# Every fourth weight tile of the first layer's experts: its second part subtracted on GpSimd instead of VectorE

## The chip, the core and the metric

The kernel runs on one core of a Trainium2 chip. Its engines work side by side, each through its own queue of instructions in program order: TensorE (PE in the profile) multiplies matrices out of SBUF into PSUM, VectorE (DVE) and ScalarE (ACT) do elementwise work, GpSimd (POOL) does elementwise work and issues indirect DMAs, SyncE (SP) issues the other DMAs. They wait for each other by semaphores. The metric is the device time of one execution in microseconds (us); before the change it is 3566.11 us, the median of three runs (3563.67 to 3567.10).

## The reference, cut to what matters

The program is two transformer blocks of two layers each, on 256 tokens of width 1024. The second block's feed-forward is a layer of 16384 experts (128 x 128). For each token, eight heads score 128 + 128 sub-keys, the best 16 of each side are combined, the best 16 sums are chosen, and the 16 experts per head are mixed:

```python
def peer_block(hb, w_q, sub_keys, u_tab, v_tab):
    ...
    top_s, pos = lax.top_k(cand_s, PEER_TOPK)
    expert = jnp.take_along_axis(cand_i, pos, axis=-1)
    g = jax.nn.softmax(top_s, axis=-1)
    u = u_tab[expert]
    act = jax.nn.gelu(jnp.einsum('nhkd,nd->nhk', u, hb).astype(jnp.float32))
    w = (g * act).astype(hb.dtype)
    return jnp.einsum('nhk,nhkd->nd', w, v_tab[expert])
```

In the first of the two layers 256 latent tokens and 256 context tokens go through it.

## The kernel before

The kernel doesn't gather experts for most tokens: it runs all 16384 experts densely, as 128 tiles of 128 experts, and multiplies with a gate matrix that is zero where an expert wasn't chosen. In the first layer (l = 0) 448 tokens go this way (N = ND = 448); the other 64 context tokens go through `gather`, which fetches two rows of experts per step with an indirect DMA from GpSimd (L1329) and multiplies them on VectorE (L1338 for `u`, L1344 for `v`). The second layer has N = S = 256 tokens.

A float32 matrix is used as two float32r parts, so that three matmuls give the precision of one float32 product: `split` writes the first part on ScalarE (L210, a copy that rounds) and the second on VectorE (L211, the source minus the first part), and `mac` issues first x first (L244), first x second (L245) and second x first (L246). A weight tile of 128 x 1024 thus costs one ScalarE and one VectorE instruction of 1024 columns, and 24 matmuls.

The first pass is `ahead`: for each tile e, `hidden` loads `u[e]` (buffer tag `w`, four buffers), splits it into two `ws` buffers of four, multiplies it with h into PSUM tag A, applies the GELU (L1146), and the result goes to DRAM (`kept`). Tiles 0 to 26 have 256 columns here, since their context half was done earlier (`fill`); tiles 27 to 127 have 448. With four `ws` buffers the parts of tile e + 2 can be written only after the matmuls of tile e.

Beside it `ahead` steps through side work at given rates: `key_scores` and `choose` (VectorE: top-16, L945 to L1043), `spread`, which builds the gate matrix, and the gather. `spread` makes a one-hot tile for every four tokens: three instructions on GpSimd and one on VectorE (L1078), three more on VectorE (L1082), eight small matmuls (L1096), a copy on ScalarE (L1097); 112 such tiles in this layer. Their buffers are the three of tag `wb`, which the loads of `v` and of the modulation weights use too.

The second pass is `experts`: for each tile, `weigh` loads `kept[e]` and `v[e]`, splits `v[e]` into a `k8` buffer of seven, multiplies the activation with its gate (L1192), splits that, and `sums` issues 24 matmuls, one tile behind, into eight PSUM banks.

The functions record instructions in program order; a scheduler of the framework then sets each engine's order by its own estimates of durations. Here are the functions around the change, with the line numbers of the profile.

Of the kernel before, what the change touches and what calls it, by code (L numbers as in the profile page):

```python
# [10 lines left out]
F32 = mybir.dt.float32  # L11
# [4 lines left out]
ALU = mybir.AluOpType  # L16
AX = mybir.AxisListType

P = 128
S = 256  # L20
D = 1024
KC = 8
# [36 lines left out]
class Net:  # L59
# [145 lines left out]
            return tuple(t if t is None or b is None else t[:, b * P:(b + 1) * P] for t in dst(k))  # L205
        return hT

    def split(self, hi, lo, src):

        self.nc.scalar.copy(hi, src)  # L210
        self.nc.vector.tensor_sub(lo, src, hi.bitcast(F32))  # L211

    def cut_in_two(self, shape, raw):

        tag = self.ring[self.turn % len(self.ring)]
        self.turn += 1
        if tag == "ws":
            hi, lo = self.t("ws", [P] + shape, F32R), self.t("ws", [P] + shape, F32R)
        else:
            both = self.t(tag, [P, 2] + shape, F32R)  # L220
            hi, lo = both[:, 0], both[:, 1]
        self.split(hi, lo, raw)
        return hi, lo

    def weights(self, sd, src, n=512, order=None):
# [906 lines left out]
    def hidden(self, l, e, h, N, aside=False):  # L1132

        nc, io = self.nc, self.io
        raw = self.load("wb" if aside else "w", [P, KC, P], io["u"][l, e])
        if aside:
            both = self.t("b8", [P, 2, KC, P], F32R)
            uh, ul = both[:, 0], both[:, 1]
            self.split(uh, ul, raw)
        else:  # L1140
            uh, ul = self.cut_in_two([KC, P], raw)
        pA = self.p("B" if aside else "A", [P, N])
        for k in range(KC):
            self.mac(pA, (uh[:, k], ul[:, k]), h(k), k == 0, k == KC - 1)
        ge = self.t("b2" if aside else "k2", [P, N])
        nc.scalar.activation(ge, pA, AF.Gelu_apprx_tanh)  # L1146
        return ge
# [24 lines left out]
    def experts(self, l, h, N, Gd, kept, side, home):  # L1172

        nc, io = self.nc, self.io
        m = 8
        pv = [self.p(t, [P, 512 if N == S else N]) for t in ("CCCC" if N == S else "CCCCBBAA")]
        Gs = None

        def weigh(e):
            nonlocal Gs
            c, j = divmod(e, m)
            if j == 0:
                Gs = self.t(home, [P, N // NT, m, NT])
                nc.sync.dma_start(Gs, Gd[:, :, m * c:m * c + m])
            ge = self.load("k2", [P, N], kept[e]) if e < kept.shape[0] else self.hidden(l, e, h, N)
            raw = self.load("wb", [P, D], io["v"][l, e])
            vs = self.t("k8", [P, 2, D], F32R)
            self.split(vs[:, 0], vs[:, 1], raw)  # L1190
            g3 = ge.rearrange("p (n t) -> p n t", t=NT)
            nc.vector.tensor_mul(g3, g3, Gs[:, :, j])  # L1192
            ws = self.t("k4", [P, 2, N], F32R)
            self.split(ws[:, 0], ws[:, 1], ge)
            return ws, vs

        def sums(i, e, ws, vs):
            w, v = ([t[:, j] for j in range(2)] for t in (ws, vs))
            if N == S:
                b, d = divmod(i, 2)  # L1200
                self.mac(pv[i], self.cut(w, b * P, (b + 1) * P), self.cut(v, 512 * d, 512 * d + 512), e == 0, e == 127)
            else:
                self.mac(pv[i], self.cut(v, i * P, (i + 1) * P), w, e == 0, e == 127)

        banks, late = range(len(pv)), []
        last = None
        for e in range(129):
            if side is not None:
                side(e)
            new = (e,) + weigh(e) if e < 128 else None  # L1210
            if e > 128 - TAIL:
                late.append(last)
            elif last is not None:
                for i in banks:
                    sums(i, *last)
            last = new
        for i in banks:
            for w in late:
                sums(i, *w)
            yield i, pv[i]  # L1220
# [345 lines left out]
```

## Time and profile before

| | |
|---|---|
| median of 3 runs | 3566.11 us (3563.67 to 3567.10) |
| the profiled execution, its span | 3569.61 us, 3567.2 us |
| TensorE matmul busy | 3375.9 us (95%) |
| VectorE, ScalarE busy | 2466.8 us (69%), 1508.8 us (42%) |
| GpSimd busy | 748.7 us (21%), in two stretches: `spread` of each layer |
| granted TensorE clock, mean | 0.976 |

The shares are means over stages with different limits. A stage is read from its own window: who is busy there, and for whom TensorE waits. A row of the grouped lines gives line, engine, operation, tiles written and read, shapes and count, then busy us, mean ns of one, and the idle time of the engine before them with what ended it. A row of the timeline gives start, duration, engine, line, and in brackets the idle time before it and its releaser.

### The profile page before, as it was taken

The page shows a single profiled execution, that of the slowest core. Times are in us where ns is not written, and L with a number is a line of the kernel's source. Part 1 is how long each engine was busy: PE and PEld are TensorE (multiplying, and loading weights), DVE is VectorE, ACT ScalarE, POOL GpSimd, SP SyncE. Part 2 cuts the span into 40 slices and gives each one's busy share as a digit, 9 for nine tenths or more (in the row PEclk, how much of TensorE's full clock was granted, in tenths as well). Part 3 has the DMA queues.
Part 4 walks back from the last instruction along what each step waited for, and adds up shares of the span by engine and source line. Part 5 has one row for each costly group of instructions (what it writes and reads, how often), then busy time and mean ns, then how long its engine had stood idle before and what let it go on. Part 6 is the DMA issues. An engine that isn't in the chain of part 4 may idle for free. (4 is left out here: it accounts for less than half of the span.)

```text
span 3567.2 us, 54493 instructions
## 1 busy us (share of the span) xinstructions
PE 3375.9 (95%) x19896; PEld 2942.5 (82%) x19896; DVE 2466.8 (69%) x5248; ACT 1508.8 (42%) x2556; POOL 748.7 (21%) x728
## 2 busy tenths in 40 slices
PE   8999999999999998999876999999989999999999
PEld 6687777799888987888765889888968999998777
DVE  6656776655667678997756765555477888756666
ACT  6543455444454433433312233233354545555443
POOL 0000000000000055988843200000010045730000
PEclk9999999999999998999998999999999999999999
DMA  7446644455524656776789977786322577788885
GB/s 242 157 159 214 208 152 136 158 201 196 169 92 147 217 198 225 256 246 217 276 302 316 331 261 246 243 251 220 109 67 103 197 243 260 252 288 287 291 273 194
DMA packets 338796, 767.05 MB, mean 215 GB/s; under 512 B 30368, under 2 KB 190624, under 8 KB 332640
## 3 DMA queue, kind: packets, MB, share of 16 engines
q1 hardware_dynamic: 320096, 696.46, 58.0%
q0 software_dynamic: 18432, 67.12, 5.3%
q8 instruction: 156, 2.56, 0.3%
q14 instruction: 112, 0.92, 0.1%
HBM read 668.50 MB, written 94.96 MB: 214 GB/s over the span
## 5 line engine op out<-in xcount | busy, mean ns | idle before, releaser
L210 ACT CAST ws<-w 128x1024 fp32r<-128x1024 f32 (+1 forms) x528 | 547.2, 1036 | 958.1 <-PE psA L245 693.0
L211 DVE TENSOR_TENSOR ws<-w,ws 128x1024 fp32r<-128x1024 f32 (+1 forms) x528 | 637.1, 1207 | 323.5 <-ACT ws L210 320.3
L246 PE MATMUL psA<-b,ws 128*128 128x256 f32 (+1 forms) x2048 | 661.4, 323 | 46.1 <-DVE ws L211 45.8
L244 PE MATMUL psA<-b,ws 128*128 128x256 f32 (+1 forms) x2048 | 667.2, 326 | 0.7 <-ACT k L1146 0.7
L245 PE MATMUL psA<-b,ws 128*128 128x256 f32 (+1 forms) x2048 | 658.0, 321 | 0.0
L1078 POOL TENSOR_SCALAR wb<-iota,R 128x128 f16<-128x128 f16 x528 | 524.3, 1007 | 459.4 <-ACT R L1049 317.6
L210 ACT CAST k<-wb 128x1024 fp32r<-128x1024 f32 x256 | 268.5, 1051 | 484.1 <-DMA wb<-in_v 480.2
L246 PEld LDWEIGHTS psA<-b,ws 128*128 128x128 f32 x2048 | 391.4, 191 | 72.5 <-DVE ws L211 57.7
L244 PE MATMUL psC<-k,k 128*128 128x512 f32 (+1 forms) x1056 | 404.8, 383 | 22.7 <-ACT k L210 22.7
L245 PE MATMUL psC<-k,k 128*128 128x512 f32 (+1 forms) x1056 | 407.0, 385 | 16.2 <-DVE k L211 16.0
L244 PEld LDWEIGHTS psA<-b,ws 128*128 128x128 f32 x2048 | 394.2, 192 | 15.1 <-ACT k L1146 1.1
L246 PE MATMUL psC<-k,k 128*128 128x512 f32 (+1 forms) x1056 | 404.1, 383 | 2.4 <-DVE k L211 2.4
L245 PEld LDWEIGHTS psA<-b,ws 128*128 128x128 f32 x2048 | 391.4, 191 | 14.0
L211 DVE TENSOR_TENSOR k<-wb,k 128x1024 fp32r<-128x1024 f32 x256 | 312.2, 1220 | 74.3 <-ACT k L210 67.8
L159 POOL TENSOR_TENSOR rsrf<-rsvf,neghalf 128x1 f32<-128x1 f32 (+5 forms) x38 | 39.6, 1049 | 1456.0 <-DVE rsvf L158 1454.8
L1192 DVE TENSOR_TENSOR k<-k,b 128x448 f32<-128x448 f32 (+1 forms) x256 | 131.5, 522 | 178.7 <-DMA k<-kept 173.2
L245 PE MATMUL psC<-ws,k 128*128 128x512 f32 (+1 forms) x608 | 242.0, 398 | 5.0 <-DVE ws L211 4.7
L244 PEld LDWEIGHTS psC<-k,k 128*128 128x128 f32 x1056 | 200.1, 190 | 56.5 <-ACT k L210 24.0
L245 PEld LDWEIGHTS psC<-k,k 128*128 128x128 f32 x1056 | 200.4, 190 | 52.4 <-DVE k L211 21.6
L244 PE MATMUL psC<-ws,k 128*128 128x512 f32 (+1 forms) x608 | 241.6, 401 | 0.7 <-ACT ws L210 0.6
L246 PE MATMUL psC<-ws,k 128*128 128x512 f32 (+1 forms) x608 | 238.9, 394 | 0.1
L246 PEld LDWEIGHTS psC<-k,k 128*128 128x128 f32 x1056 | 200.4, 190 | 36.8 <-DVE k L211 5.0
(445 smaller groups left out, 6597.8 us busy)
## 6 DMA issues: line engine op xcount, KB each, us to landing
w<-in_u SPq DMA_DIRECT2D x256, 512.0 KB
wb<-in_v SPq DMA_DIRECT2D x256, 512.0 KB
w<-in_w_ff SPq DMA_DIRECT2D x128, 512.0 KB
G<-k SPq DMA_DIRECT2D x44, 1024.0 KB
wb<-in_ada_w SPq DMA_DIRECT2D x80, 512.0 KB
b<-G SPq DMA_DIRECT2D x16, 1792.0 KB
k<-kept SPq DMA_DIRECT2D x128, 224.0 KB
w<-in_wA SPq DMA_DIRECT2D x48, 512.0 KB
```

The lines of the kernel that those rows point to most:

```text
L159: nc.gpsimd.tensor_tensor(r[:m, :cols], v[:m, :cols], self.neghalf[:m, :cols], op=ALU.pow)
L210: self.nc.scalar.copy(hi, src)
L211: self.nc.vector.tensor_sub(lo, src, hi.bitcast(F32))
L244: self.nc.tensor.matmul(out, ah, bh, start=first, stop=False)
L245: self.nc.tensor.matmul(out, ah, bl, start=False, stop=False)
L246: self.nc.tensor.matmul(out, al, bh, start=False, stop=last)
L1078: eng.tensor_scalar(first[:, j], self.iota16, r0[:, n + j:n + j + 1], None, ALU.is_equal)
L1192: nc.vector.tensor_mul(g3, g3, Gs[:, :, j])
```

## The change

`split` gets a flag `far` that puts its subtraction on GpSimd; `hidden` and `weigh` set it for every fourth tile of the layer with 448 columns (`N > S`). Tiles 0 to 26 of the first pass and the whole second layer keep VectorE. 26 subtractions of `u` and 32 of `v` move.

```diff
-    def split(self, hi, lo, src):
+    def split(self, hi, lo, src, far=False):
 
         self.nc.scalar.copy(hi, src)
-        self.nc.vector.tensor_sub(lo, src, hi.bitcast(F32))
-
-    def cut_in_two(self, shape, raw):
+        (self.nc.gpsimd if far else self.nc.vector).tensor_tensor(lo, src, hi.bitcast(F32), op=ALU.subtract)
+
+    def cut_in_two(self, shape, raw, far=False):
...
-        self.split(hi, lo, raw)
+        self.split(hi, lo, raw, far)
         return hi, lo
...
-            uh, ul = self.cut_in_two([KC, P], raw)
+            uh, ul = self.cut_in_two([KC, P], raw, N > S and e % 4 == 3)
...
-            self.split(vs[:, 0], vs[:, 1], raw)
+            self.split(vs[:, 0], vs[:, 1], raw, N > S and e % 4 == 3)
```

GpSimd's queue beside `spread` of the third block of tokens, at tile 75 of the first pass (`ws_15141` is its second part, `ws_15140` its first, `w_15138` the raw tile; `wb_...` are one-hot tiles, `k_2265` and `b_2264` the places of the gathered rows):

```order
 L1078 TENSOR_SCALAR wb_15086<-iota_225,R_2588_14770 128x128 x3
 L1078 TENSOR_SCALAR wb_15113<-iota_225,R_2588_14770 128x128 x3
+L211 TENSOR_TENSOR ws_15141<-w_15138,ws_15140 128x1024
+L1329 DMA k_2265_12552<-in_u_rows,idx_12187 128x1024 x2
 L1329 DMA b_2264_12551<-in_u_rows,idx_12187 128x1024
 L1078 TENSOR_SCALAR wb_15172<-iota_225,R_2588_14770 128x128 x3
-L1329 DMA k_2265_12552<-in_u_rows,idx_12187 128x1024
 L1078 TENSOR_SCALAR wb_15197<-iota_225,R_2588_14770 128x128 x3
```

The subtraction stands behind the one-hot tile `wb_15113`, and the row gathers around it have moved: one that stood between the next two one-hot tiles is gone from there, and two stand right behind the subtraction.

The same queue at tile 87 (`ws_16099`, its second part). TensorE's own order, unchanged here, has the matmuls of tile 87 ahead of those with `wb_16071` and `wb_16133`:

```order
 L1078 TENSOR_SCALAR wb_16071<-iota_225,R_2588_14770 128x128 x3
 L1078 TENSOR_SCALAR wb_16133<-iota_225,R_2588_14770 128x128 x3
+L211 TENSOR_TENSOR ws_16099<-w_16096,ws_16098 128x1024
 L1078 TENSOR_SCALAR wb_16156<-iota_225,R_2588_14770 128x128 x3
 L1078 TENSOR_SCALAR wb_16212<-iota_225,R_2588_14770 128x128 x3
```

Nothing else moved at this place: the six GpSimd instructions of the two one-hot tiles stand ahead of the subtraction.

GpSimd's queue after `spread`, beside the gather, at tile 123 of the first pass (`ws_18212`) in the new order, where the old one has the gathers alone:

```order
 L1329 DMA b_2264_12551<-in_v,idx_12187 128x1024
 L1329 DMA k_2265_12552<-in_v,idx_12187 128x1024
+L211 TENSOR_TENSOR ws_18212<-w_18209,ws_18211 128x1024
+L1329 DMA k_2265_12552<-in_v,idx_12187 128x1024
+L1329 DMA b_2264_12551<-in_v,idx_12187 128x1024
```

Each gather behind the subtraction now also waits until that one has had its first part from ScalarE and is done.

## Rows read from the trace of the kernel before

**Rows 1.** The page: busy time of each engine, share of the span, instructions.

```profile
PE 3375.9 (95%) x19896; PEld 2942.5 (82%) x19896; DVE 2466.8 (69%) x5248; ACT 1508.8 (42%) x2556; POOL 748.7 (21%) x728
```

**Rows 2.** Windows: length, busy PE, PEld, DVE, ACT, POOL; clock, DMA, GB/s.

```profile
1232.00:1396.00 164.00, 148.25 (x783) 131.32 (x781) 125.25 (x401) 51.90 (x80) 70.11 (x68) 0.95 0.62 211
1396.00:1763.00 367.00, 339.17 (x2080) 290.44 (x2081) 328.75 (x957) 139.62 (x218) 330.13 (x318) 0.97 0.69 241
1763.00:1915.00 152.00, 112.33 (x478) 96.86 (x477) 87.81 (x90) 31.86 (x45) 72.10 (x58) 0.89 0.83 290
1915.00:2480.00 565.00, 530.01 (x2553) 481.40 (x2552) 356.42 (x487) 170.01 (x224) 33.89 (x23) 0.97 0.82 269
```

**Rows 3.** TensorE's waits in the four windows: us in total, times, longest.

```profile
PE psC L1096 <- DVE k L1018: 8.1, 1, 8.1
PE psA L246 <- DVE ws L211: 6.7, 5, 4.5
...
PE psC L1096 <- POOL wb L1078: 23.0, 33, 2.8
PE psA L246 <- DVE ws L211: 3.5, 6, 1.4
...
PE psA L246 <- DVE ws L211: 35.2, 14, 6.2
...
PE psC L244 <- ACT k L210: 18.4, 1, 18.4
PE psC L245 <- DVE k L211: 16.0, 11, 5.6
```

**Rows 4.** Grouped lines of GpSimd and VectorE in 1396 to 1763.

```profile
L1078 POOL TENSOR_SCALAR wb<-iota,R 128x128 f16<-128x128 f16 x284 | 286.0, 1021 | 28.5 <-issue 25.0 <-PE psC L1096 2.5
...
L211 DVE TENSOR_TENSOR ws<-w,ws 128x1024 fp32r<-128x1024 f32 x55 | 67.8, 1232 | 10.1 <-ACT ws L210 10.0
```

**Rows 5.** L1078 by line in that window (ns min/median/max); GpSimd's smallest two-input operation.

```profile
L1078 POOL TENSOR_SCALAR wb<-iota,R x284: 590/748/4240, 1396.3 to 1763.0; 128x128 f16<-128x128 f16 x142
...
L159 POOL TENSOR_TENSOR rsrf<-rsvf,neghalf 128x1 f32<-128x1 f32 x16 | 10.0, 632 | 1109.5 <-DVE rsvf L158 1108.3 <-DVE rsvb L158 1.1
```

**Rows 6.** Timeline at tile 75: GpSimd, VectorE, TensorE.

```profile
1532.49 4.24 POOL L1078 TENSOR_SCALAR wb<-iota,R 128x128 f16<-128x128 f16 x1
...
1533.25 1.22 DVE L211 TENSOR_TENSOR ws<-w,ws 128x1024 fp32r<-128x1024 f32 x1
...
1535.06 1.21 DVE L1338 SCALAR_TENSOR_TENSOR b<-k,b 128x1024 bf16<-128x1024 f32 x1
...
1534.52 0.47 PE L246 MATMUL psA<-b,ws 128*128 128x448 f32 x1 [0.45 <-DVE ws L211]
```

**Rows 7.** Grouped lines of VectorE in 2050 to 2480.

```profile
L211 DVE TENSOR_TENSOR k<-wb,k 128x1024 fp32r<-128x1024 f32 x88 | 107.3, 1220 | 13.3 <-ACT k L210 13.3
```

**Rows 8.** Timeline at tile 87: GpSimd, TensorE.

```profile
1618.43 2.25 POOL L1078 TENSOR_SCALAR wb<-iota,R 128x128 f16<-128x128 f16 x2
...
1614.48 0.36 PE L246 MATMUL psA<-b,ws 128*128 128x448 f32 x1
```

**Rows 9.** Timeline at tile 103: GpSimd, TensorE.

```profile
1717.58 1.68 POOL L1078 TENSOR_SCALAR wb<-iota,R 128x128 f16<-128x128 f16 x1
...
1717.20 0.36 PE L246 MATMUL psA<-b,ws 128*128 128x448 f32 x1
```

**Rows 10.** Timeline at tile 126, beside the gather: ScalarE, VectorE.

```profile
1888.90 1.05 ACT L210 CAST ws<-w 128x1024 fp32r<-128x1024 f32 x1 [3.43 <-PE psA L245]
...
1898.69 1.29 DVE L1344 SCALAR_TENSOR_TENSOR b<-b,act 128x1024 f32<-128x1024 f32 x1 [4.80 <-DMA b<-in_v,idx]
1899.89 1.22 DVE L211 TENSOR_TENSOR ws<-w,ws 128x1024 fp32r<-128x1024 f32 x1
```

**Rows 11.** Timeline at tile 19 of the second pass: VectorE, TensorE.

```profile
2029.14 1.22 DVE L211 TENSOR_TENSOR k<-wb,k 128x1024 fp32r<-128x1024 f32 x1
...
2033.55 0.37 PE L246 MATMUL psC<-k,k 128*128 128x448 f32 x1
```

## The prediction

> **What bounds the kernel now.** I read the page's busy line first: TensorE is busy for 3375.9 of 3567.2 us [rows 1], so the change can only give back, or add to, some 190 us of idle TensorE time. It acts between 1232 and 2480 us (the layer-0 expert work at 448 columns), so I cut that into four stages by the view of windows [rows 2]. A, 1232 to 1396: expert tiles 27 to 53 beside the last choosing of keys. B, 1396 to 1763: tiles 54 to 109 beside `spread`. C, 1763 to 1915: tiles 110 to 127 beside the gather. D, 1915 to 2480: the second pass, where the tiles of `v` are split. TensorE idles 16, 28, 40 and 35 us in them. The view of waits by stage says for whom [rows 3]: in B 23.0 us for GpSimd's one-hot tiles (L1078) and only 3.5 us for VectorE's second weight part; in C 35.2 us for that second part; in A 6.7 us for it and 8.1 us once for VectorE's choosing; in D 18.4 us once at the stage's start and 16.0 us for the second part of the gated activations, which isn't moved.
>
> In B three engines are nearly full: TensorE 339, VectorE 329, GpSimd 330 of 367 us [rows 2]. The grouped lines of B show why GpSimd is so full: its 284 instructions of L1078 take 1021 ns in the mean [rows 4], though the shortest took 590 ns [rows 5]. One of them shows where the rest goes [rows 6]: it runs 4.24 us while VectorE works through one operation with two SBUF inputs after the other, the last ending at 1536.27, and ends half a us after that. So a GpSimd instruction stands still while VectorE does such work. VectorE hardly suffers from it: L211 takes 1232 ns in B [rows 4] and 1220 ns after the gather, where GpSimd does nothing [rows 7].
>
> **The change, part by part.** 58 subtractions of 128x1024 leave VectorE for GpSimd: 26 of `u` (tiles 27, 31, ... 127) and 32 of `v`. VectorE loses 58 x 1.22 us = 71 us. No row has this operation on GpSimd. From below: a two-input GpSimd operation on one element takes 632 ns [rows 5], so nearly all of the shortest L1078 may be a fixed cost, and a subtraction would take little over 0.6 us. From above: if nothing of the 590 ns is fixed, eight times as many elements take 4.7 us. L1078 is the nearest row for both ends and doesn't say how much is fixed; I take half way, 2.65 us, and add the 0.43 us by which an L1078 in B is longer than the shortest, so 3.1 us (ends 1.0 and 5.1). The Trainium skill (GPSIMD Engine Reference, Performance versus the Vector engine) states 4497 ns for 2048 elements; half of that with the same 0.43 us makes an estimate of 2.7 us, and the sum below 5 us smaller. No row here shows it.
>
> *Stage B*, 14 tiles (55 to 107). GpSimd works in program order, and the order puts the subtraction of a tile behind one-hot tiles that TensorE wants only after that tile. So I set, for each, the end of the GpSimd work ahead of it (or of ScalarE's first part, if later) plus 3.1 us against TensorE's first matmul with the second part. Three of them: tile 75 stands behind the one-hot tile whose last instruction ends at 1536.73 [rows 6]; 1536.7 + 3.1 = 1539.8 against 1534.52, a stall of 5.3 us. Tile 87: its first part is ready in time, but ahead of it on GpSimd stand two one-hot tiles, the later of which ends at 1620.68; 1623.8 against 1614.48, 9.3 us [rows 8]. Tile 103: GpSimd ends at 1719.26; 1722.4 against 1717.20, 5.2 us [rows 9]. Read in the same way, nine others give 0.8 to 4.3 us and tiles 63 and 95 nothing; two of the nine (55, 107) don't stall by themselves but push late one-hot tiles by 3.1 us. The fourteen make 40.7 us. Not all of it stays: once TensorE is late, the 26.5 us that it waits in B today partly vanish, and VectorE's 14 missing subtractions no longer hold up L1078. I take back half of the 26.5: 13. Net +27.7 us. At the ends of the price the fourteen make 19.4 and about 66 us, net +6 and +53.
>
> *Stage A*, seven tiles. GpSimd is free for most of them (70 of 164 us busy [rows 2]), and VectorE's work on the critical choosing gets 8.5 us shorter. TensorE's two waits of 6.7 and 8.1 us lose at best 8.5; two subtractions land some 1 us late (tiles 27 and 35), so I take -3 us.
>
> *Stage C*, five tiles. Here the first part of tile 126 is done at 1889.95, but its second starts at 1899.89: VectorE's queue stood at L1344 for a gathered row, 4.80 us alone [rows 10]. On GpSimd a subtraction passes that block. Five of the stage's eighteen tiles move, so 5/18 of the 35.2 us, 9.8, could go. I take half: GpSimd's own row gathers stand between them and wait for L1344 too. And each subtraction, which itself waits for ScalarE's first part, delays the gathers queued behind it by 3 us or more, and VectorE's L1344 after them. -5 us.
>
> *Stage D*, 32 tiles. The split of `v` has room: the smallest lead of the 32 is that of tile 19, done at 2030.36 and first used at 2033.55 [rows 11], 3.2 us later, and VectorE's queue had held it up; GpSimd is busy 34 of D's 565 us [rows 2]. What hides these 32 is that lead; without it each would cost the 1.9 us by which 3.1 exceeds 1.22. Raw tiles come free a little earlier, since GpSimd doesn't wait for `kept` as VectorE does, but TensorE isn't waiting for those loads. 0 us.
>
> Queues moved past: some fifty of SyncE's loads and stores trade places with a neighbour, and the gather's fetches come later by two or three in B, since the order now counts GpSimd as fuller; the gather's sums are needed only after D. I cost both at nothing; if the gather slid far, it would be VectorE's block of stage C that lasts longer.
>
> Sum: -3 + 27.7 - 5 + 0 = +20 us. The profiled execution took 3569.6 us, its span 3567.2 and 2.4 around it, so 3590; it lies 3.5 us over the median 3566.1, which puts a median at 3586. With the ends of the price: 3564 to 3611.
>
> **Rivals.** *Relief wins.* VectorE is the fullest engine but TensorE in A and as full as GpSimd in B (125 of 164, 329 of 367 us [rows 2]), its lag causes GpSimd's, and C's waits are all VectorE's. If GpSimd's subtraction is short (near 1 us) and the later order of the row gathers lets it keep up, the stalls in B come to no more than the waits they replace; what remains is A at its best, C's 9.8 and B's 3.5: -8.5 - 9.8 - 3.5 = -22 us, 3544. It decides from a price below about 1.3 us. For it: those waits are real. Against it: TensorE's slack against VectorE in B is ample (3.5 us of waits) and against GpSimd there is none (23.0).
>
> *A wash.* Stalls in B just take the place of today's 26.5 us, since three full engines settle on a common pace: half the stalls vanish, A and C give 8: 20 - 13 - 8, within a few us of 3566.
>
> *GpSimd holds VectorE up.* If a long GpSimd read, once begun, stops VectorE's two-input work till it ends, VectorE gains 1.22 us per tile and loses up to 2.65: in B 14 x 1.4 = 20 us on an engine that is 90% full, on top of the forecast: 3606. Against it stand the 12 ns by which L211 is longer in B, but those GpSimd reads have 128 elements. The Trainium skill (SBUF — State Buffer, Who interferes with whom) speaks for it: whichever starts first has the shared ports for its whole instruction, and the other blocks. The trace shows the blocking of GpSimd by VectorE (4.24 us); the other way it shows only those 12 ns.
>
> That the change doesn't do what it says is excluded by the order, which has 58 new rows on GpSimd and those 58 gone from VectorE.
>
> **How the numbers follow.** Forecast 0.52, GpSimd holding VectorE up 0.10, relief 0.20, a wash 0.18. What a measurement of this kernel can tell from no change is about 0.2%, 7 us. Of the forecast's own range (3564 to 3611) about a sixth lies below 3573, so slower is 0.52 x 5/6 + 0.10 + a sixth of the wash = 0.56; the wash and that sixth leave 0.22 for same; faster is relief and a little of the wash, 0.22. The range must reach to relief on one side and past 3606 on the other: 3546 to 3616, with about a tenth left out at each end. The forecast's own is 3564 to 3611.
>
> **What would show it.** In the new profile L211 on GpSimd has 58 instructions of 128x1024; their duration in D, where VectorE is less busy, gives the price, and that in B what VectorE adds. In B TensorE's waits for `ws` should be on GpSimd L211, some 25 to 40 us, tile 87's the longest, and the stage 25 to 30 us longer than 367. In C the waits for L211 should fall by about 5 us. L1078 should be shorter than 1021 ns if VectorE's absence helps it. The forecast is wrong if B isn't longer, or if D is: then the lead of the `v` tiles was no cover. GpSimd holding VectorE up would show as L211 on VectorE well over 1232 ns in the mean.

## The result, and the profile after

The changed kernel takes 3603.39 us (median of 6 runs, 3589.72 to 3612.53) beside 3566.61 us for the kernel before on the same chip (6 runs): a ratio of 1.0094, 95% interval 1.0074 to 1.0114. It is slower by 36.8 us between the medians and by some 33 us by the ratio: the forecast's sign, and 13 to 17 us more than its +20. The profiled execution has a span of 3609.1 us, 41.9 over that of before; it is one of the longest of its six runs.

The page's busy line of the changed kernel:

```profile
PE 3388.1 (94%) x19896; PEld 2954.1 (82%) x19896; DVE 2483.8 (69%) x5190; ACT 1509.2 (42%) x2556; POOL 877.7 (24%) x786
```

Two things differ from [rows 1] in a way to stop at. VectorE lost 58 subtractions of 1.22 us, 71 us of work, and yet is busy for 17 us *more*. And TensorE, with the same 19896 matmuls, is busy 12.2 us longer: the mean granted clock is 0.970 where it was 0.976. So of the 41.9 us some 30 are new idle time of TensorE and 12 are matmuls that ran at a lower granted clock.

The four stages, cut at the same work as in [rows 2] (columns as there):

```profile
1233.00:1415.00 182.00, 152.40 (x786) 134.65 (x786) 130.93 (x400) 52.64 (x80) 85.59 (x78) 0.92 0.59 198
1415.00:1804.00 389.00, 348.11 (x2114) 301.09 (x2112) 331.74 (x943) 143.51 (x225) 351.85 (x334) 0.94 0.65 229
1804.00:1946.00 142.00, 107.87 (x441) 93.54 (x442) 82.97 (x79) 26.87 (x38) 75.90 (x54) 0.86 0.84 289
1946.00:2525.00 579.00, 534.98 (x2552) 482.86 (x2552) 367.78 (x462) 170.04 (x224) 104.73 (x53) 0.97 0.80 262
```

In A and B the granted clock is 0.92 and 0.94 (0.95 and 0.97 in [rows 2]); in D VectorE is busy 11 us longer though 27 subtractions left this window. TensorE's waits in the four windows (total, times, longest), to set against [rows 3]:

```profile
PE psA L246 <- DVE ws L211: 15.6, 5, 5.3
PE psC L1096 <- DVE k L1018: 10.8, 1, 10.8
PE psA L246 <- POOL ws L211: 2.5, 2, 2.2
...
PE psA L246 <- POOL ws L211: 12.4, 4, 4.8
PE psC L1096 <- POOL wb L1078: 11.8, 15, 4.3
PE psC L1096 <- DVE wb L1082: 10.0, 4, 7.7
...
PE psA L246 <- DVE ws L211: 29.4, 10, 5.4
PE psA L246 <- POOL ws L211: 4.7, 3, 2.7
...
PE psC L245 <- DVE k L211: 24.1, 13, 5.8
PE psC L244 <- ACT k L210: 18.7, 1, 18.7
```

Only 19.6 us of these waits name the moved subtraction. In A the wait for *VectorE's own* second parts has grown from 6.7 to 15.6 us, and in D that for the second part of the activations, which nobody moved, from 16.0 to 24.1. So the change makes VectorE late for work that it kept. A's window, for one, is 18 us longer (182 against 164): 8.9 more for VectorE's second parts, 2.5 for the moved ones, 2.7 more for the choosing (L1018: 10.8 against 8.1), and 4.2 of matmuls at the lower clock. In B TensorE's waits for GpSimd (L1078 and L211 together) are 24.2 us, where L1078 alone had 23.0: they hardly grew. What GpSimd's subtraction itself takes, by line (ns min/median/max):

```profile
L211 POOL TENSOR_TENSOR k<-wb,k x32: 2391/2476/3262, 1973.1 to 2606.8; 128x1024 fp32r<-128x1024 f32 x32
L211 POOL TENSOR_TENSOR ws<-w,ws x26: 2330/2408/3085, 1231.4 to 1938.4; 128x1024 fp32r<-128x1024 f32 x26
```

For the rest of the text the stages are cut by TensorE's own rows: A from the first matmul of tile 27 to that of tile 54, B from there to tile 110, C from there to the first matmul of the second pass, D the whole second pass. One profiled execution each, in us:

| kernel | A | B | C | D |
|---|---|---|---|---|
| before | 164.3 | 377.4 | 162.1 | 655.7 |
| after | 181.6 | 389.6 | 162.7 | 670.0 |
| e1: u only | 181.4 | 389.4 | 157.6 | 655.3 |
| e2: v only | 164.5 | 376.5 | 161.8 | 664.7 |
| e3: u in A | 181.6 | 380.1 | 162.2 | 656.9 |
| e4: u in B | 164.2 | 390.4 | 164.4 | 652.9 |
| e5: spare subtraction in D | 164.7 | 385.6 | 161.8 | 679.2 |
| e14: copy in D | 164.7 | 380.3 | 162.4 | 656.1 |
| e6: spare subtraction in A | 169.2 | 384.2 | 162.4 | 650.8 |
| e10: before, no gather | 143.2 | 343.7 | 99.5 | 636.1 |
| e11: after, no gather | 143.8 | 346.8 | 102.7 | 644.3 |
| e12: before, five places | 159.9 | 382.4 | 135.4 | 651.1 |
| e13: after, five places | 172.8 | 385.9 | 134.1 | 665.8 |
| e7: u in C, all | 162.4 | 376.8 | 157.7 | 662.6 |

Where nothing moved in a stage, A lies within 162.4 and 164.7, B within 376.5 and 385.6, D within 650.8 and 662.6: that is the table's own scatter, and only A is sharp. For D above all, the runs' medians have to decide.

### The profile page after: what moved, and what is told of

Same layout as the page of the kernel before. It is cut to its first block, busy times and chain, and to the rows that moved or that the text cites. A ratio compares the mean times of both kernels' runs of the same rounds, so it can differ in the third digit from the quotient of the medians.

```text
span 3609.1 us, 54544 instructions
## 1 busy us (share of the span) xinstructions
PE 3388.1 (94%) x19896; PEld 2954.1 (82%) x19896; DVE 2483.8 (69%) x5190; ACT 1509.2 (42%) x2556; POOL 877.7 (24%) x786
## 5 line engine op out<-in xcount | busy, mean ns | idle before, releaser
L211 DVE TENSOR_TENSOR ws<-w,ws 128x1024 fp32r<-128x1024 f32 (+1 forms) x502 | 604.8, 1205 | 324.8 <-ACT ws L210 321.1
L1078 POOL TENSOR_SCALAR wb<-iota,R 128x128 f16<-128x128 f16 x528 | 506.7, 974 | 295.4 <-ACT R L1049 158.6
L245 PE MATMUL psC<-k,k 128*128 128x512 f32 (+1 forms) x1056 | 408.7, 387 | 24.8 <-DVE k L211 24.1
L211 DVE TENSOR_TENSOR k<-wb,k 128x1024 fp32r<-128x1024 f32 x224 | 272.9, 1219 | 58.0 <-ACT k L210 51.4
L1192 DVE TENSOR_TENSOR k<-k,b 128x448 f32<-128x448 f32 (+1 forms) x256 | 168.9, 668 | 178.7 <-DMA k<-kept 170.9
```

What stands on the lines that cost most here:

```text
L211: (self.nc.gpsimd if far else self.nc.vector).tensor_tensor(lo, src, hi.bitcast(F32), op=ALU.subtract)
L245: self.nc.tensor.matmul(out, ah, bl, start=False, stop=False)
L1078: eng.tensor_scalar(first[:, j], self.iota16, r0[:, n + j:n + j + 1], None, ALU.is_equal)
```

## The experiments

### Where the time goes: e1 to e4

The changed kernel with one part of the change each; the flag at the two calls:

```diff
 e1, e2:  -  N > S and e % 4 == 3      + False          (at v; at u)
 e3:      at u  N > S and e % 4 == 3 and e < 54          (at v False)
 e4:      at u  N > S and e % 4 == 3 and 54 <= e < 110   (at v False)
```

> Only the 26 subtractions of u go to GpSimd, those of v stay on VectorE. The stages of the changed kernel's trace are longer than before's by 17 (A), 12 (B), 1 (C) and 14 us (D). Stages add up (theory 'each move pays at its own place'): about +30 us, 3597, and D as before (some 656 us from first to last first-part matmul). My forecast's working (A -3, B +28, C -5): +20, 3587. If D's loss comes from what the first pass leaves behind (a late gather, late stores) and not from v: about +44, 3610, with D at 670.

> Only the 32 subtractions of v go to GpSimd. If they cost what stage D lost: +14 us, 3581, stages A to C as before, and L1192 on VectorE well over its 522 ns mean of before (theory 'GpSimd's read holds VectorE up'). If the lead covers them, as forecast: 3566 within 7, D at 656. If D's loss came from the first pass: the same as forecast, though L1192 may be longer.

> Only the seven subtractions of u tiles 27 to 51 go to GpSimd (stage A). Theory 'late fetch' (the row gathers queued behind a subtraction come late, VectorE stands at L1338 and its own weight parts behind it are late): about +17 us in A, some of it given back where B's waits for GpSimd shrink; 3575 to 3583. Theory 'GpSimd holds VectorE up': seven times at most 2.4 us, so at most +17 too, but then without a wait of VectorE for rows over before's 2.3 us. My forecast's working: -3 us, 3563.

> Only the fourteen subtractions of u tiles 55 to 107 go to GpSimd (stage B). By the changed kernel's stage B: +12 us, 3578. My forecast's working at the price now seen (2.4 us in place of 3.1, so 14 x 0.7 less of stalls): about +18, 3584. 'Three full engines settle on a pace' (a wash): within 7 us of 3566.

Measured against before (3569.59 us): e1 3590.75, ratio 1.0059 (1.0042 to 1.0076); e2 3576.99, 1.0023 (1.0011 to 1.0035); e3 3580.16, 1.0030 (1.0020 to 1.0040); e4 3586.49, 1.0054 (1.0035 to 1.0072). So u costs 21 us and v 7, 28 of the 33 together. e1's 21 us are near the +20 of the forecast's working, but its stages are not: A is 17 us longer, B 12, and C 4.5 shorter. D's loss is v's: the medians of e2 show a cost that is there with u left alone, and its D is longer, as e1's is not (e2's 664.7 alone would show little beside the 662.6 of e7). A's 17 us are there in each of the three kernels that move its seven tiles, and in none that doesn't; over the whole kernel they come to 10.6 us, so some is given back, or this execution was a long one. B alone costs 17 us by the medians, 12 to 13 by the stage, whose own scatter is 9. Each of A, B and D loses, and no stage wins what would pay for another.

### D: what a GpSimd read does to VectorE (e5, e14)

The rows of the changed kernel at the subtraction of v tile 19, GpSimd and then VectorE (start, duration, engine, line):

```profile
2063.45 2.59 POOL L211 TENSOR_TENSOR k<-wb,k 128x1024 fp32r<-128x1024 f32 x1 [8.94 <-ACT k L210]
...
2063.69 2.83 DVE L1192 TENSOR_TENSOR k<-k,b 128x448 f32<-128x448 f32 x1
```

VectorE's L1192 starts 0.24 us after GpSimd's subtraction, takes 2.83 us where this shape takes 0.62, and ends 0.48 us after it. The grouped lines of L1192 at 448 columns, of before and then of after (busy, mean ns):

```profile
L1192 DVE TENSOR_TENSOR k<-k,b 128x448 f32<-128x448 f32 x128 | 77.8, 622 | 115.3 <-DMA k<-kept 115.2
```

```profile
L1192 DVE TENSOR_TENSOR k<-k,b 128x448 f32<-128x448 f32 x128 | 115.4, 915 | 121.5 <-DMA k<-kept 119.2 <-issue 1.7 <-DVE k L211 0.2
```

32 subtractions of 1.22 us went away, 39 us, and this one line took 37.6 of them back. Over all stages, taking each VectorE record that overlaps a moved subtraction and the median of its shape from it, 48 instructions were held up for 82 us together (34.6 in A to C, 47.3 in D); 71 had been taken off. So what VectorE gave away came back as standing still, and its busy time rose.

Is it the holding, or the later second part of v? In e5 VectorE does every subtraction, and GpSimd does one that nobody reads; in e14 GpSimd only copies. `split` in both, with the flag at v alone (shortened at the marks <...>):

```diff
         self.nc.scalar.copy(hi, src)
         self.nc.vector.tensor_sub(lo, src, hi.bitcast(F32))
+        if far: self.nc.gpsimd.tensor_tensor(<spare b2 tile, bf16>, src, hi.bitcast(F32), op=ALU.subtract)   # e5
+        if far: self.nc.gpsimd.tensor_copy(<spare b2 tile, bf16>, hi.bitcast(F32))                           # e14
```

> VectorE keeps all its subtractions; for every fourth v tile GpSimd makes the same subtraction once more into a spare bf16 tile (tag b2) that TensorE never reads. Theory 'GpSimd's read holds VectorE up': the 32 extra reads of 2.4 us stretch VectorE's L1192 and L211 as with v moved, so stage D loses at least what it lost with v alone (some 9 us in its trace, 664.7 against 655.7), and more, since VectorE keeps the 39 us: +8 to +20 us, 3574 to 3590. Theory 'late second part' (the subtraction on GpSimd is 1.2 us longer and TensorE waits for it): nothing waits for the spare tile, so 3566 within 5, D at 656.

> As the kernel with the spare subtraction in D, but GpSimd only copies the first part into the spare tile, one input instead of two. If any GpSimd read of this size holds VectorE up: L1192 on VectorE reaches over 2 us again and D is 10 to 23 us longer than 655.7 in proportion to the copy's duration, total +6 to +16. If two inputs are what it takes: L1192 stays under 0.7 us, D within 3 us of 656, total within 5 us of 3566.

e5: 3589.93 against 3569.40, ratio 1.0044 (1.0028 to 1.0060), so 16 us by the ratio and 20 between the medians, with D at 679.2 us. Nothing reads the spare tile, so the lateness of v's second part isn't needed for the cost: GpSimd's read is enough. It does two things, though: it holds VectorE up, and it keeps the raw tile, whose buffer the next loads want. The second is small where it can be read: SyncE's loads (L119) waited for the spare subtraction twice, 4.4 us in all, and five times, 13.3 us, for the moved ones in the changed kernel. The grouped lines of e5:

```profile
L1192 DVE TENSOR_TENSOR k<-k,b 128x448 f32<-128x448 f32 x128 | 115.8, 918 | 112.0 <-DMA k<-kept 111.9
L212 POOL TENSOR_TENSOR b<-wb,k 128x1024 bf16<-128x1024 f32 x32 | 86.6, 2706 | 482.2 <-ACT k L210 482.2
```

And of e14:

```profile
L1192 DVE TENSOR_TENSOR k<-k,b 128x448 f32<-128x448 f32 x128 | 89.2, 711 | 113.4 <-DMA k<-kept 113.0
L212 POOL CAST b<-k 128x1024 bf16<-128x1024 f32 x32 | 45.4, 1418 | 494.3 <-ACT k L210 494.3
```

e14: 3574.01 against 3577.62, ratio 0.9997 (0.9983 to 1.0011), D at 656.1. Neither of its expectations held whole: L1192 is held up, by 11.4 us in sum and to 1.46 us at most, so one input is enough for that; but the time doesn't move. The copy differs from e5's subtraction in three things, its one input, its 1.4 us in place of 2.7, and that it doesn't read the raw tile; which of them spares the time, no run tells.

How the holding reaches TensorE is not the short way that one expects. TensorE waits in D for VectorE's second part of the activations (24.1 us after, 16.0 in [rows 3]), which follows L1192 on VectorE. But of the 24.1 us only 4.0, in three places, follow a held-up instruction with no idle time of VectorE in between. 9.8 stand behind L778, where VectorE had waited for a modulation weight (8.9 before), and 10.2 behind L1344, where it had waited for a gathered row (5.6 before). Two such places, before and then after:

```profile
2126.81 1.23 DVE L778 SCALAR_TENSOR_TENSOR b<-wb,kv 128x1024 bf16<-128x1024 f32 x1 [8.48 <-DMA wb<-in_ada_w]
2128.64 0.74 PE L245 MATMUL psC<-k,k 128*128 128x448 f32 x1 [2.17 <-DVE k L211]
```

```profile
2168.18 1.22 DVE L778 SCALAR_TENSOR_TENSOR b<-wb,kv 128x1024 bf16<-128x1024 f32 x1 [9.31 <-DMA wb<-in_ada_w]
2170.01 0.47 PE L245 MATMUL psC<-k,k 128*128 128x448 f32 x1 [2.92 <-DVE k L211]
```

In e5 some 18 of 30 us stand behind L778 in this way, and 9 behind a held-up instruction. That a VectorE which is held up also frees tiles later, so that loads come later, would explain it; no run shows that path by itself.

### A and B: the gather (e10, e11)

At tile 36 the changed kernel has these rows, GpSimd, VectorE, TensorE:

```profile
1271.25 2.41 POOL L211 TENSOR_TENSOR ws<-w,ws 128x1024 fp32r<-128x1024 f32 x1
1273.84 1.20 POOL L1329 DMA_INDIRECT b<-in_u_rows,idx  x1 [0.18 <-issue]
...
1271.60 2.35 DVE L1082 TENSOR_TENSOR wb<-iota,R 128x512 f16<-128x512 f16 x1
...
1280.34 1.22 DVE L1338 SCALAR_TENSOR_TENSOR b<-b 128x1024 bf16<-128x1024 f32 x1 [5.60 <-DMA b<-in_u_rows,idx]
...
1282.93 1.20 DVE L211 TENSOR_TENSOR ws<-w,ws 128x1024 fp32r<-128x1024 f32 x1
...
1284.19 0.74 PE L246 MATMUL psA<-b,ws 128*128 128x448 f32 x1 [5.27 <-DVE ws L211]
```

The same place before:

```profile
1269.45 1.20 POOL L1329 DMA_INDIRECT b<-in_u_rows,idx  x1 [0.19 <-issue]
...
1274.27 1.22 DVE L1338 SCALAR_TENSOR_TENSOR b<-b 128x1024 bf16<-128x1024 f32 x1 [2.27 <-DMA b<-in_u_rows,idx]
...
1276.86 1.21 DVE L211 TENSOR_TENSOR ws<-w,ws 128x1024 fp32r<-128x1024 f32 x1
...
1278.12 0.47 PE L246 MATMUL psA<-b,ws 128*128 128x448 f32 x1 [1.23 <-DVE ws L211]
```

The first row fetch stood right behind the one-hot tiles; now it stands behind the subtraction of tile 35. VectorE comes to L1338 and waits 5.60 us for the row in place of 2.27, and the second part of tile 36, on VectorE as before, stands behind that. TensorE's wait grows from 1.23 to 5.27 us. At tile 52 a second thing is added:

```profile
1388.12 2.41 POOL L211 TENSOR_TENSOR ws<-w,ws 128x1024 fp32r<-128x1024 f32 x1 [1.28 <-ACT ws L210]
1390.67 1.77 POOL L1329 DMA_INDIRECT k<-in_u_rows,idx  x1
...
1388.79 0.27 DVE L945 MAX8 k<-k 128x8 f32<-128x128 f32 x1
1388.98 2.62 DVE L1338 SCALAR_TENSOR_TENSOR b<-k,b 128x1024 bf16<-128x1024 f32 x1
...
1397.22 1.23 DVE L1338 SCALAR_TENSOR_TENSOR b<-k,b 128x1024 bf16<-128x1024 f32 x1 [4.21 <-DMA k<-in_u_rows,idx]
...
1401.37 1.22 DVE L211 TENSOR_TENSOR ws<-w,ws 128x1024 fp32r<-128x1024 f32 x1
```

Of the three L1338 here the first is held up (2.62 us for 1.2), and the last waits for a row whose fetch went out behind the subtraction. VectorE's order changed as well: the scheduler, presumably because it counts VectorE as freer, has moved L1338s up; 20 of them lie in A in place of 18 (VectorE's order around L1029, against before):

```order
+L1338 SCALAR_TENSOR_TENSOR b2_2421_13601,act_2266_12553<-k8_2265_12552,b8_2264_12551 128x1024
 L1029 TENSOR_TENSOR k2_2351_13144<-k8_2211_12199,c_iota_211 128x1024
...
 L211 TENSOR_TENSOR ws_2374_13290<-w_2372_13287,ws_2373_13289 128x1024
-L1338 SCALAR_TENSOR_TENSOR b2_2421_13601,act_2266_12553<-k8_2265_12552,b8_2264_12551 128x1024
```

The L1338 that writes b2_2421 stood behind a later subtraction and stands ahead of L1029 now, which is the row behind the last L1338 at tile 52.

To see whether the gather carries A's and B's loss, e10 and e11 are before and after without it (`fetch` and the multiplications left out, `acc` set to zero).

> The kernel before without the gather: its 128 row fetches on GpSimd and the 128 multiplications on VectorE (L1338, L1344) are left out, so the 64 context tokens get no expert sum. A base for the next kernel. VectorE loses some 155 us of work and its blocks at the rows: C's 35 us of waits and some of A's go, 3520 to 3555.

> The changed kernel without the gather, left out as in the kernel without it above; their difference is the change's price when no row fetch stands behind a subtraction and no multiplication of rows in VectorE's queue. Theory 'late fetch and moved multiplications' for A: A's +17 vanishes, the difference is B's and D's, +12 to +27. Theory 'GpSimd holds VectorE up' for A and B too: about +30 as with the gather. Theory 'late behind one-hot tiles' for B: B still loses 12 or more with TensorE's waits on GpSimd's L211; if B's loss too is the gather's, the difference is D's alone, +8 to +14.

e10 takes 3425.53, e11 3448.87 (0.9589 and 0.9657 of before's 3569.40; intervals 0.9566 to 0.9612 and 0.9640 to 0.9675). My bound for e10 was far off: the gather costs 144 us, not 15 to 50. The change now costs 23.3 us, and the table says where: A 0.7, B 3.1, C 3.1, D 8.2 (the rest of the two spans' 20.9 us, some 6, lies in the layer behind, which is the same in both). So A's 17 us need the gather, or the 150 us of work that it puts on VectorE, and most of B's 12 do; D's don't. For B this answers the forecast's own theory: the subtractions stand behind one-hot tiles in e11 too, and B, which was to lose 12 or more by it, loses 3.1, with one wait of 2.5 us for a moved subtraction. Holding by itself doesn't make A's loss either: in e11 it stretches VectorE's instructions by 25 us in A to C, and TensorE doesn't feel it. Beside the gather, where VectorE is fuller, e11 says nothing of it.

### Late fetch or moved multiplications: e6, e12, e13

e6 is e5's `split` with the flag at u for e < 54. e12 (before) and e13 (changed) give the gather five places and fetch four steps ahead:

```diff
-        hr, two = self.t("b8", [P, 2, D]), self.t("k8", [P, 2, D])
+        hr, two, more = self.t("b8", [P, 2, D]), self.t("k8", [P, 2, D]), self.t("k8", [P, 2, D])
...
-        places = hr[:, 1], two[:, 0], two[:, 1]
+        places = hr[:, 1], two[:, 0], two[:, 1], more[:, 0], more[:, 1]
...
-            fetch(i + 2)
+            fetch(i + 4)
```

> VectorE keeps all its subtractions; in stage A, for tiles 27, 31, ... 51, GpSimd makes the same subtraction once more into a spare bf16 tile (tag b2) that TensorE never reads. A took 164.3 us before and 181.6 with the seven subtractions moved; without the gather moving them cost A 0.7. Theory 'late fetch' (the row fetches stand behind a GpSimd instruction that itself waits for ScalarE): they stand behind the spare one too, so A is 10 to 20 us longer than 164.3. Theory 'moved multiplications' (the order, counting VectorE as freer, puts L1338 ahead of the second parts): VectorE is counted as full as before, so A stays within 3 us of 164.3.

> The kernel before with five places for gathered rows instead of three, so that each fetch is issued four steps ahead instead of two (a k8 buffer is taken for it). A base for the next kernel. If VectorE's waits for rows (some 99 us in all at L1338 and L1344) come from fetches issued late: 10 to 40 us faster, 3526 to 3556, and C well below 162. If they come from the transfers' rate (C moves 290 GB/s): within 7 us of 3566, or slower by the buffer that is missing.

> The changed kernel with five places for gathered rows. Theory 'late fetch': a fetch four steps ahead can bear a delay of some 5 us, so A's +17 shrinks to under 5 and the price of the change against the kernel with five places above falls from 33 to what it is without the gather, 15 to 25. Otherwise the price stays at 30 to 40 and A at +17.

e6: 3580.84 against 3577.62, ratio 1.0017 (1.0003 to 1.0031), A at 169.2. That is 4.9 us over 164.3, under the 10 to 20 that late fetches alone should have cost and over the 3 that the other theory allowed. But the 4.9 is a net. TensorE's wait for second parts in A is as long as in the changed kernel (15.6 and 2.5; 6.7 before), tile 36 with 4.45 us among it:

```profile
PE psA L246 <- DVE ws L211: 17.6, 9, 5.7
```

What e6 lacks is the one wait for the choosing (L1018), 8.1 us before and 10.8 in the changed kernel, and the low clock (0.96 in A; 0.92 changed). Its order isn't that of before either: 16 L1338 lie in A. So the fetch behind GpSimd's instruction and the holding, together, are enough for the late second parts, with every subtraction on VectorE.

e12: 3537.10 against 3577.62, ratio 0.9894 (0.9871 to 0.9917): a version 1.1% faster than before, at the upper end of its first expectation, and the best of those that do all the work. C falls from 162.1 to 135.4 us. Its windows, before and then e12:

```profile
1773.40:1935.40 162.00, 108.03 (x452) 93.03 (x449) 96.55 (x95) 32.03 (x45) 72.53 (x54) 0.85 0.86 300
```

```profile
1775.00:1910.00 135.00, 95.98 (x452) 83.89 (x449) 97.58 (x94) 32.67 (x47) 72.71 (x59) 0.89 1.01 380
```

With more rows under way the same stage moves 380 GB/s in place of 300.

e13: 3569.16, ratio 0.9980 (0.9968 to 0.9993) to before, but 32 us over e12. The theory of late fetches said that its price would fall to 15 to 25 us; it didn't. A still costs 12.9 us (172.8 against 159.9): the first fetch is late whatever the depth (tile 36 waits 5.30), and at tile 52, now without any wait for rows, TensorE waits 3.60 us behind three L1338. VectorE's rows of e13 there:

```profile
1384.26 1.20 DVE L1338 SCALAR_TENSOR_TENSOR b<-k,b 128x1024 bf16<-128x1024 f32 x1
...
1385.67 1.19 DVE L1338 SCALAR_TENSOR_TENSOR b<-b 128x1024 bf16<-128x1024 f32 x1
...
1386.80 1.21 DVE L1338 SCALAR_TENSOR_TENSOR b<-k,b 128x1024 bf16<-128x1024 f32 x1
...
1390.94 1.21 DVE L211 TENSOR_TENSOR ws<-w,ws 128x1024 fp32r<-128x1024 f32 x1
```

So A's loss needs the gather; the second parts are late with a read on GpSimd ahead of the fetches even where nothing is moved (e6), and more places take away some 4 of A's 17.2 us. Whether VectorE's new order adds to it, by L1338s ahead of second parts or of the choosing, is argued and not shown: no run kept the old order with the moved subtractions, and e6 changed the order too.

### C: e7

`far` at u for `N > S and e >= 110`: all eighteen.

> All eighteen u tiles from 110 on (stage C) have their second part written by GpSimd, nothing else moves. Theory 'passes the block' (VectorE's queue stands at L1344 for gathered rows, a subtraction on GpSimd passes it): of C's 35 us of waits a good part goes, -10 to -20 us, 3546 to 3556. Theory 'late fetch' (the row fetches behind a subtraction come late and GpSimd's own subtraction stands behind fetches that wait for VectorE): the waits only change their name, within 7 us of 3566, or up to +10.

3571.20 against 3569.40, ratio 1.0004 (0.9992 to 1.0016): no change. C is 4.4 us shorter, D 6.9 longer with nothing moved in it, and where [rows 3] had 35.2 us of waits for VectorE stand 30.5 for GpSimd:

```profile
PE psA L246 <- POOL ws L211: 30.5, 17, 2.9
```

GpSimd's fetches wait for VectorE's L1344 (26.4 us in C), and the subtraction stands behind them: the waits mostly changed their name, as the second expectation had it.

## Why the prediction was right or wrong

**Right: the sign, and that B loses; not how it loses.** B was to lose 27.7 us at a price of 3.1 us for a subtraction; the price was 2.44 in B, so some 20 by the same working. e4 measured 17 by the medians, and by the stage 12 to 13. That these are near is luck, for the picture is not the one drawn. Of fourteen stalls of 40.7 us four are left, 12.4 us, where the forecast's sign for it was 25 to 40. Tile 87, for which 9.3 us were worked out, waits 4.76:

```profile
1634.42 8.93 POOL L1078 TENSOR_SCALAR wb<-iota,R 128x128 f16<-128x128 f16 x7
1643.32 2.87 POOL L211 TENSOR_TENSOR ws<-w,ws 128x1024 fp32r<-128x1024 f32 x1
...
1646.25 0.74 PE L246 MATMUL psA<-b,ws 128*128 128x448 f32 x1 [4.76 <-POOL ws L211]
```

This is the mechanism, a subtraction behind one-hot tiles. Tile 75 was to wait 5.3 and doesn't wait, because TensorE is late there for other reasons. The waits for L1078 fell from 23.0 to 11.8, near the 13 that I took back, and its mean from 1021 to 966 ns. So the term "stalls less what vanishes", +27.7 on paper, came to some +1. Grown, from 4.6 to 10.0, is the wait for VectorE's L1082, and 7.7 of it is one place, just ahead of tile 75's matmuls, where VectorE stood 4.49 us for a row ahead of its one-hot work:

```profile
1563.51 1.68 DVE L1338 SCALAR_TENSOR_TENSOR b<-k,b 128x1024 bf16<-128x1024 f32 x1 [4.49 <-DMA k<-in_u_rows,idx]
...
1567.21 0.75 DVE L1082 TENSOR_TENSOR wb<-wb,R 128x512 f16<-128x512 f16 x2
```

That is the gather again, and fits e11, where B loses 3.1 and not 12. The step that failed: my stalls were set against other suppliers that stay where they were. How the rest of B's loss parts between late rows, held-up VectorE work and the lower clock (0.94 for 0.97) no run tells.

**Wrong: A, -3, measured +17 in the stage and +10.6 in the time.** The step that failed is the one on the queues: I counted what GpSimd's subtraction is queued behind, and put what is queued behind *it* at nothing ("I cost both at nothing"). The row fetches behind it come late, VectorE waits for the rows, and the second parts that stand behind that on VectorE are late: this is what A pays for (without the gather it loses 0.7 us). A slide of the gather I had set only into C. What the L1338s that the order moved up add, stays open.

**Wrong: D, 0, measured +8 to +14 in the stage and +7 in the time (e2).** That D is longer was one of the prediction's own signs of being wrong. "What hides these 32 is that lead" held for the second part of v, whose lead of 3.2 us [rows 11] bears 1.3 us more: TensorE never waits for it. The step that failed is that nothing but this lead was asked after. GpSimd's reads of 2.6 us hold VectorE up, by 47.3 us in D, and the second part of the activations, which has no such lead, is late: 24.1 us of waits for 16.0. The matmuls, at the lower clock, add 5. This is the rival *GpSimd holds VectorE up*, which had a chance of 0.10, and I set its price into B, where no run sets it apart, and not into D. Against it I had 12 ns from reads of 128 elements [rows 4, 7], which is no evidence on reads of 1024. The Trainium skill (SBUF — State Buffer, Who interferes with whom) had it: two VectorE inputs against a GpSimd read, whoever starts first keeps the ports for the whole instruction. The trace agrees: L1338 with two inputs took 2.62 us at 1388.98 and MAX8 with one took 0.27 beside the same subtraction. Who was first the trace doesn't always tell: six of the 48 held-up instructions start up to 0.49 us ahead of GpSimd's. The instrument for it was named (VectorE's mean duration), but on the wrong line: the weight tiles' L211 on VectorE stayed at 1.22 us, and L1192 went from 622 to 915 ns.

**C, -5:** -4.5 and -4.4 in the stages of e1 and e7, +0.6 in the changed kernel, nothing in e7's time. The size was met in two stages, one of them with eighteen tiles moved in place of five, and it reached no kernel's time.

**The price,** 2.65 us without VectorE's share, measured 2.33 at the shortest: inside the bounds of 0.6 and 4.7, near the half way that was taken. The 0.43 us for VectorE's share were too much: 2.44 in the mean in B. The Trainium skill's figure (GPSIMD Engine Reference, Performance versus the Vector engine; half of 4497 ns, an estimate of 2.25 us) was the closer one.

**The sum** was right in sign because B's term carries it, and that term has the right sign by a working that mostly didn't happen; that the sum came within 13 to 17 us is luck, for A and D, which cost some 18 us between them by the medians of e3 and e2, stood in it with -3 and 0. Also left out was the clock: TensorE's matmuls ran 12.2 us longer in all, which no term of mine had.

## What to carry to other kernels

Moving work from VectorE to GpSimd can save VectorE nothing if it reads large inputs while VectorE has two-input work (here 71 us went and 82 came back): count the GpSimd instruction's whole duration as a possible stop of VectorE, and look what stands behind the stopped instruction and which loads wait for the tiles that it frees. On a queue that issues DMAs, cost what stands *behind* the new instruction before what stands ahead of it. And where an engine waits for gathered rows, more places to fetch into can be worth more than any shift of work: two more gave 1.1% here.

## What the runs showed of the hardware

- GpSimd's subtraction of two 128x1024 float32 inputs takes 2.33 us at the shortest and 2.41 to 2.48 in the median; its copy of one such input to bf16 1.04 at the shortest, 1.42 in the mean; it holds L1192 up as well, to 1.46 us.
- A VectorE instruction with two SBUF inputs that starts inside such a subtraction does its whole work after it: L1082 ends 0.29 us behind GpSimd's end, L1192 0.48, L1338 1.07, each 0.13 or 0.14 us less than its own undisturbed duration (0.42, 0.62, 1.20). Its one-input searches (MAX8, FIND_INDEX8) pass; four L1078 and a conversion (L1010), with one tensor input each, were held up too, by 2.1 to 2.6 us.
- Five row fetches in place of three raised the traffic of a stage from 300 to 380 GB/s, with the DMA engines' busy share at 1.01 (0.86 with three).
- The gather takes 150 us of VectorE's 2467 and costs 144 us of the kernel, though TensorE is the fullest engine: without it TensorE is busy 3328.7 us at a granted clock of 0.989 (3375.9 at 0.976 before), and waits some 95 us less.
